# Two places instead of one between each sum of the RWKV-7 state chain and the product that reads it

## The chip, the cores and the metric

The kernel runs on one core of a Trainium2 chip. The metric is the device time of one launch in microseconds (us). Work is shared by TensorE (PE, matrix products), VectorE (DVE), ScalarE (ACT), GpSimd (POOL) and SyncE (SP, which issues most of the transfers).

## The reference

One layer of a hybrid decoder on 256 prompt tokens and 8 decode tokens, T = 264 columns, in 32-bit floats: a SwiGLU feed-forward block, a mixing layer in which attention heads and RWKV-7 heads stand side by side, a second SwiGLU block, and norms. The part that matters here is the RWKV-7 recurrence over the 256 prompt tokens, 16 heads of 64:

```python
def step(S, inp):
    r_t, lw_t, k_t, v_t, kk_t, a_t = inp
    sa = jnp.einsum('bhij,bhj->bhi', S, -kk_t)
    S = (S * jnp.exp(lw_t)[:, :, None, :] + sa[..., None] * (kk_t * a_t)[:, :, None, :]
         + v_t[..., None] * k_t[:, :, None, :])
    return S, jnp.einsum('bhij,bhj->bhi', S, r_t)
S, ys = lax.scan(step, S0.astype(jnp.float32), xs)
```

## The kernel before

All large products are weight products. `gemm` (its products have line 74 in the profile) goes through a weight tile in chunks of four 128 x 128 blocks: SP loads a chunk (`raw`), ScalarE rounds it to the fast product format (`hi`, line 127), VectorE or GpSimd forms the remainder (`lo`, line 58), and TensorE makes three products for each block, `hi` by `xh`, `hi` by `xl` and `lo` by `xh`, twelve for a chunk, each over 264 columns, into an `acc` bank of PSUM. There are 6 `raw`, 4 `hi` and 4 `lo` buffers, 3 `acc` banks and 5 banks with the tag `m` for all smaller products.

Between the two feed-forward blocks lies the mixing layer. Its projection `win` computes 38 tiles of 128 columns: tiles for the RWKV heads, then 4 tiles of keys and values, then 8 tiles of queries; after it the output projection (`in_wout`) adds in three passes. For the query tiles and the output projection the `lo` parts alternate between GpSimd and VectorE.

The smaller work of the mixing layer is written as Python generators in a list `tasks`. After each chunk, `gemm` calls `tick`, which lets every task in the list run on to its next `yield`. So a `yield` is a place in the program at which one chunk of products, and a step of every other task, stands between two parts of a task; `pause(n)` is n such places:

```python
def pause(n):
    for _ in range(n):
        yield
```

The tasks are: `prep`, one for each of 8 pairs of heads (decays, norms, the matrices within a block of 64 tokens); `chain`, one for each batch of two pairs, four in all; and `attend`, `dec_attend`, `dec_load` and `kvtask` for attention. The output projection waits (`drain`) for the tasks whose results a pass needs; `dec_load(1, ...)`, which starts the second decode attention, waits for the last chain.

`chain` first inverts triangular matrices (30 steps of two VectorE instructions, which write `st` and `Xt`), then forms, by products and copies, what the recurrence over four blocks of 64 tokens needs: `PT` (the map of a state over a block), `kr` (what reads the state), and, in the banks pN and pY, what each block adds to the state and the output by itself. Then comes the state chain, four sums with products between them: `N` scales pN; for c = 1, 2, 3 the products by `PT` and by `kr` read the state so far (`N` for c = 1, then `S`), and `S` is formed from it in two steps, `Z` (line 61) and `S` (line 61). Last, the outputs in pY are copied, the state is written (`out_wkvp`, line 697, issued by ScalarE's queue), `g2` is loaded and `gnorm` normalises the output.

The order in which each engine executes is not the program's: a planner assigns it, from a model of when operands are ready, and with the place in the program as priority. `tc.high_priority()` lifts the `hi` and `lo` steps of a chunk ahead of older work. Every engine then executes its own list in order, so an instruction that has to wait holds up what stands behind it.

Of the kernel before, what the change touches and what calls it, by code (L numbers as in the profile page):

```python
# [47 lines left out]
def body(tc, I, O):  # L48
# [11 lines left out]
    def stt(out, a, s, b, op0, op1):  # L60
        return V.scalar_tensor_tensor(out=out, in0=a, scalar=s, in1=b, op0=op0, op1=op1)  # L61
# [8 lines left out]
    def bc(ap, shape):  # L70
        return ap.broadcast_to(list(shape))

    def mm(out, lhsT, rhs, start=True, stop=True, **k):
        TE.matmul(out, lhsT, rhs, start=start, stop=stop, **k)  # L74
# [16 lines left out]
# [4 lines that stand above are left out]
    with ExitStack() as ctx:  # L95
# [17 lines left out]
        def mp():  # L113
            return pp.tile([P, 512], F32, tag="m", bufs=NM, name=uid("m"))
# [245 lines left out]
        def mixing_body(mx, n2, n3, XD):  # L360
# [3 lines left out]
            def ring(shape, tag, bufs):  # L364
                return mx.tile(list(shape), F32, tag=tag, bufs=bufs, name=uid(tag))
# [182 lines left out]
            def chain(bt):  # L548
# [114 lines left out]
                for k in range(n):  # L663
# [5 lines left out]
                               k + c == 0, c == 0, skip_group_check=True)  # L669
                tt(V, N, pN[:, :n * 256].rearrange("p (k c t) -> p k c t", k=n, c=4),  # L670
                   bc(wc[:, bt.p0:bt.p0 + n, :].unsqueeze(3), (P, n, 4, 64)), ALU.mult)
                yield
                S = N[:, :, 0, :]
                for c in range(1, 4):
                    ps = mp()
                    for k in reversed(range(n)):
                        for h in range(2):
                            r = HALF[h]
                            mm(ps[r, k * 64:k * 64 + 64], PT[r, k, c - 1, :], S[r, k])
                        for h in range(2):  # L680
                            r = HALF[h]
                            x = (k * 4 + c) * 64
                            mm(pY[HALF[1 - h], x:x + 64], S[r, k], bt.KR[k][r, 1, c, :], False, True,
                               skip_group_check=True)
                    Z, Sn = ring((P, n, 64), "Z", 2), ring((P, n, 64), "S", 3)
                    for k in range(n):
                        stt(Z[:, k], S[:, k], wc[:, bt.p0 + k, c:c + 1], N[:, k, c, :], ALU.mult, ALU.add)
                    for k in range(n):
                        stt(Sn[:, k], ps[:, k * 64:k * 64 + 64], wc[:, bt.p0 + k, c:c + 1], Z[:, k], ALU.mult, ALU.add)
                    S = Sn  # L690
                    yield
                for k in range(n):
                    for h in range(2):
                        A.copy(Ys[k][HALF[h], :NP], pY[HALF[1 - h], k * NP:(k + 1) * NP])
# [182 lines left out]
            for kind, i in SEQ:  # L877
                if kind == "b":
                    bt = newbatch(i)
                    for k in range(BATCH[i]):  # L880
                        p = bt.p0 + k
                        x = [shifted(2 + 3 * p + j, tmp()) for j in range(3)]
                        spawn(prep(p, bt, k, *x))
                    bat.append(spawn(chain(bt)))
                    bts.append(bt)
                    if len(bat) == len(BATCH):
# [206 lines left out]
```

## Time and profile before

| | |
|---|---|
| time, median of 3 runs | 1982.82 us (1982.39 to 1985.37) |
| the profiled execution | 1982.98 us, span 1981.2 us |
| busy: PE / DVE / ACT / POOL | 1960.8 / 1302.9 / 1064.1 / 347.8 us |
| the four state chains, first sum N at | 922.1, 993.5, 1047.8, 1117.8 us |
| projection and mixing layer, about | 700 to 1212 us of the span |

A time before an instruction is its start within the span. An entry of the list of waits gives who waited, for whom, microseconds in total, times, and the longest. In the order of time a bracket is the idle time of the engine just before the row, and the instruction that ended it by the profile; a product's end is modelled, so that products overlap in the rows.

### The profile page before, as it was taken

How to read it: one execution, taken by the hardware profiler on the slowest of the kernel's cores; microseconds unless marked ns; L12 is line 12 of the kernel's file. 1: busy time of each engine (PE TensorE's matmuls, PEld its weight loads, DVE VectorE, ACT ScalarE, POOL GpSimd, SP SyncE). 2: the span in 40 equal slices, each digit the busy share in tenths (PEclk: the TensorE clock that was granted, in tenths of full speed). 3: DMA queues.
4: the chain of work that ended last, by engine and by line, in shares of the span. 5: the costliest groups of instructions: out<-in, count | busy, mean ns of one | idle time of the engine just before them, and what ended most of it. 6: DMA issues, size and time to landing. Idle time of an engine off the chain costs nothing.

```text
span 1981.2 us, 45886 instructions
## 1 busy us (share of the span) xinstructions
PE 1960.8 (99%) x17212; PEld 1931.5 (97%) x17212; DVE 1302.9 (66%) x2542; ACT 1064.1 (54%) x2125; POOL 347.8 (18%) x453
## 2 busy tenths in 40 slices
PE   9999999999999999999999999999999999999997
PEld 9999999999999999999998899999999999999997
DVE  5865555655556567788877776866666666666655
ACT  5644444444444456777665755644444444444445
POOL 0401102010010112132133562210101001010112
PEclk9999999999999999999999999999999999999998
DMA  7666666665656667555656456565666666666664
GB/s 230 177 185 199 185 190 193 182 186 177 185 179 182 182 186 233 162 159 139 167 154 170 134 155 195 175 181 178 193 184 192 182 194 188 185 191 184 195 179 142
DMA packets 224880, 358.24 MB, mean 181 GB/s; under 512 B 38264, under 2 KB 79888, under 8 KB 224656
## 3 DMA queue, kind: packets, MB, share of 16 engines
q1 hardware_dynamic: 218768, 349.20, 59.7%
q10 hardware_dynamic: 5888, 6.11, 1.0%
q8 instruction: 135, 2.21, 0.4%
q14 instruction: 89, 0.73, 0.1%
HBM read 347.06 MB, written 10.22 MB: 180 GB/s over the span
## 4 chain that ended last, share of the span: by engine, by line
PE 96%; DVE 1%; DMA 1%; ACT 1%; issue 0%; SPq 0%; POOL 0%; DVEq 0%; ACTq 0%; POOLq 0%
PE acc L74 88%; PE m L74 7%; DMA raw<-in_gu 1%; DVE lo L58 0%; DVE Xt L58 0%; DVE st L58 0%; DMA TT<-sb 0%; DVE y L58 0%; DMA raw<-in_wout 0%; DMA raw<-in_win 0%; ACT t L68 0%; PE m L786 0%; PE m L522 0%; ACT L68 0%; ACT hi L127 0%
## 5 line engine op out<-in xcount | busy, mean ns | idle before, releaser
L127 ACT CAST hi<-raw 128x512 fp32r<-128x512 f32 (+2 forms) x1304 | 779.0, 602 | 809.5 <-PE acc L74 724.1
L58 DVE TENSOR_TENSOR lo<-raw,hi 128x512 fp32r<-128x512 f32 (+1 forms) x1248 | 854.6, 688 | 538.6 <-ACT hi L127 511.3
L74 PE MATMUL acc<-s,hi 128*128 128x264 f32 x5940 | 1109.1, 286 | 2.2 <-ACT hi L127 1.1
L74 PEld LDWEIGHTS acc<-s,hi 128*128 128x128 f32 x5940 | 923.1, 188 | 8.5 <-ACT hi L127 1.8
L74 PE MATMUL acc<-s,lo 128*128 128x264 f32 x2970 | 846.8, 286 | 0.3 <-DVE lo L58 0.2
L74 PEld LDWEIGHTS acc<-s,lo 128*128 128x128 f32 x2970 | 558.3, 188 | 3.6 <-issue 0.9
L74 PE MATMUL acc<-t,hi 128*128 128x264 f32 x2752 | 502.8, 284 | 0.0
L74 PEld LDWEIGHTS acc<-t,hi 128*128 128x128 f32 x2752 | 426.0, 188 | 0.0
L74 PE MATMUL acc<-t,lo 128*128 128x264 f32 x1376 | 388.7, 284 | 0.0
L58 POOL TENSOR_TENSOR t<-t,t 128x264 f32<-128x264 f32 (+1 forms) x148 | 151.1, 1021 | 1148.6 <-ACT hi L127 882.2
L74 PEld LDWEIGHTS acc<-t,lo 128*128 128x128 f32 x1376 | 258.1, 188 | 0.1
L74 PE MATMUL acc<-y,hi 128*128 128x264 f32 x648 | 123.9, 284 | 0.0
L74 PEld LDWEIGHTS acc<-y,hi 128*128 128x128 f32 x648 | 100.9, 188 | 0.2
L74 PE MATMUL acc<-y,lo 128*128 128x264 f32 x324 | 91.9, 284 | 0.0
L58 DVE TENSOR_TENSOR t<-acc,t 128x264 f32<-128x264 f32 x156 | 67.3, 432 | 36.2 <-PE acc L74 36.0
L58 POOL TENSOR_TENSOR lo<-raw,hi 128x512 fp32r<-128x512 f32 x56 | 73.6, 1316 | 57.4 <-ACT hi L127 36.0
L58 POOL TENSOR_TENSOR o<-o,o 128x264 f32<-128x264 f32 x43 | 36.1, 841 | 187.5 <-ACT o L68 183.5
L74 PE MATMUL acc<-o,hi 128*128 128x264 f32 x324 | 62.1, 281 | 0.0
L74 PEld LDWEIGHTS acc<-y,lo 128*128 128x128 f32 x324 | 60.9, 188 | 0.0
L61 DVE SCALAR_TENSOR_TENSOR s<-acc,s 128x264 f32<-128x264 f32 x96 | 40.5, 426 | 16.0 <-PE acc L74 15.5
L74 PEld LDWEIGHTS acc<-o,hi 128*128 128x128 f32 x324 | 49.9, 188 | 0.0
L74 PE MATMUL m<-s,hi 128*128 128x264 f32 x260 | 48.1, 285 | 0.0
(251 smaller groups left out, 1336.4 us busy)
## 6 DMA issues: line engine op xcount, KB each, us to landing
raw<-in_gu SPq DMA_DIRECT2D x688, 256.0 KB, 3.4
raw<-in_dn SPq DMA_DIRECT2D x224, 256.0 KB, 2.9
raw<-in_win SPq DMA_DIRECT2D x152, 256.0 KB, 3.5
raw<-in_dn SPq DMA_DIRECT2D x160, 192.0 KB, 2.7
raw<-in_wout SPq DMA_DIRECT2D x48, 256.0 KB, 3.3
raw<-in_wout SPq DMA_DIRECT2D x32, 128.0 KB, 3.0
s<-xsp SPq DMA_DIRECT2D x16, 132.0 KB, 3.8
ld<-in_sT SPq DMA_DIRECT2D x16, 128.0 KB, 3.7
```

Of the source, the lines that this page charges most:

```text
L58: return e.tensor_tensor(out=out, in0=a, in1=b, op=op)
L61: return V.scalar_tensor_tensor(out=out, in0=a, scalar=s, in1=b, op0=op0, op1=op1)
L74: TE.matmul(out, lhsT, rhs, start=start, stop=stop, **k)
L127: A.copy(hi[:, :w], raw[:, :w])
```

## The change

In `chain`, the `yield` after `N` and the `yield` at the end of each of the three rounds become `yield from pause(2)`. Nothing else changes: the instructions, their operands, the buffers and the loads stay as they are.

```diff
                 tt(V, N, pN[:, :n * 256].rearrange("p (k c t) -> p k c t", k=n, c=4),
                    bc(wc[:, bt.p0:bt.p0 + n, :].unsqueeze(3), (P, n, 4, 64)), ALU.mult)
-                yield
+                yield from pause(2)
                 S = N[:, :, 0, :]
                 for c in range(1, 4):
                     ps = mp()
...
                     for k in range(n):
                         stt(Sn[:, k], ps[:, k * 64:k * 64 + 64], wc[:, bt.p0 + k, c:c + 1], Z[:, k], ALU.mult, ALU.add)
                     S = Sn
-                    yield
+                    yield from pause(2)
```

## The prediction

> **What bounds the kernel now.** I read the page's busy line first, then the list of TensorE's waits, then the order of time around the sums of the state chain, then granted clock by short windows.
>
> ```profile
> PE 1960.8 (99%) x17212; PEld 1931.5 (97%) x17212; DVE 1302.9 (66%) x2542; ACT 1064.1 (54%) x2125; POOL 347.8 (18%) x453
> ...
> PE m L74 <- DVE st L58: 3.6, 1, 3.6
> PE m L74 <- DVE Xt L58: 2.2, 2, 1.2
> ```
>
> TensorE (PE) is busy 99% of the span, so a change that adds and removes no product can only give back time in which TensorE stands. The list of its waits (total us, times, longest) has about ten microseconds in the whole run; the two largest entries, 5.8 us, name VectorE (DVE). The next rows show where they lie: the sum N of each of the four chains, and the first products that read it. The bracket is TensorE's idle time before the row.
>
> ```profile
> 922.06 0.68 DVE L58 TENSOR_TENSOR N<-m,wc 128x512 f32<-128x512 f32 x1
> 922.89 0.27 PE L74 MATMUL m<-N,PT 64*64 64x64 f32 x2 [1.03 <-DVE Xt L58]
> ...
> 993.53 0.68 DVE L58 TENSOR_TENSOR N<-m,wc 128x512 f32<-128x512 f32 x1
> 994.36 0.27 PE L74 MATMUL m<-N,PT 64*64 64x64 f32 x2 [1.22 <-DVE Xt L58]
> ...
> 1047.81 0.68 DVE L58 TENSOR_TENSOR N<-m,wc 128x512 f32<-128x512 f32 x1
> 1048.64 0.27 PE L74 MATMUL m<-N,PT 64*64 64x64 f32 x2 [3.60 <-DVE st L58]
> ...
> 1117.76 0.69 DVE L58 TENSOR_TENSOR N<-m,wc 128x512 f32<-128x512 f32 x1 [0.41 <-PE m L74]
> 1119.91 0.27 PE L74 MATMUL m<-N,PT 64*64 64x64 f32 x2
> ```
>
> The releaser that is named (Xt, st: the doubling steps of the next batch's inverse) is only VectorE's instruction beside it; the product waits for N, which ends 0.15 us before it (1047.81 + 0.68 = 1048.49). Three chains pay 1.03, 1.22 and 3.60 us; the fourth pays nothing. The third pays twice, as the windows show (stretch, length, busy time of TensorE, weight load, DVE, ACT, POOL, then granted clock, DMA share, GB/s):
>
> ```profile
> 922.00:923.00 1.00, 0.11 (x5) 0.14 (x9) 1.00 (x5) 1.00 (x1) 0.00 (x0) 1.00 0.00 0
> 993.00:994.00 1.00, 0.14 (x2) 0.00 (x0) 0.91 (x4) 0.98 (x2) 0.21 (x2) 1.00 0.54 152
> 1049.00:1050.00 1.00, 1.00 (x14) 0.73 (x9) 0.90 (x6) 0.37 (x1) 0.00 (x0) 0.84 1.03 408
> 1050.00:1051.00 1.00, 1.00 (x9) 0.70 (x5) 1.00 (x5) 0.00 (x0) 0.70 (x1) 0.50 0.48 184
> 1051.00:1052.00 1.00, 1.00 (x6) 1.00 (x5) 1.00 (x8) 0.00 (x0) 0.20 (x1) 0.50 0.07 18
> 1052.00:1053.00 1.00, 1.00 (x6) 1.00 (x6) 1.00 (x8) 0.26 (x1) 0.00 (x0) 0.50 0.58 154
> 1053.00:1054.00 1.00, 1.00 (x22) 0.85 (x21) 0.93 (x5) 1.00 (x4) 0.51 (x1) 0.95 0.26 97
> ```
>
> In the first and second chain the granted clock stays at 1.00 across the wait. After the 3.60 us it falls to one half: the clock missing from 1.00 adds up to 0.16 + 3 x 0.50 + 0.05 = 1.71 us of work. So the three waits cost 1.03 + 1.22 + 3.60 + 1.71 = 7.56 us, and that is the ceiling of what later products can give back.
>
> **The change, part by part.** No instruction is added or removed. Of the four sums of each chain (N, then S for c = 1, 2, 3) each is now followed by two places where other work is put into the program, not one. A place is worth one chunk of the projection that is running: twelve products, three every 0.365 us by the next two rows, so 1.46 us, and whatever the other tasks emit there.
>
> ```profile
> 1043.78 0.28 PE L74 MATMUL acc<-s,lo 128*128 128x264 f32 x1
> ...
> 1044.14 0.28 PE L74 MATMUL acc<-s,lo 128*128 128x264 f32 x1
> ...
> 923.90 0.47 DVE L61 SCALAR_TENSOR_TENSOR S<-m,wc,Z 128x64 f32<-128x64 f32 x2
> ...
> 926.55 0.27 PE L74 MATMUL m<-S,PT 64*64 64x64 f32 x2
> ...
> 1125.13 0.47 DVE L61 SCALAR_TENSOR_TENSOR S<-m,wc,Z 128x64 f32<-128x64 f32 x2
> ...
> 1126.76 0.27 PE L74 MATMUL m<-S,PT 64*64 64x64 f32 x2
> ```
>
> *After S, c = 1 and 2.* The first S shown ends at 924.37, 2.18 us ahead of its product; the last, the nearest of all, 1.16 us ahead. None of these products has idle time in front. I take 0 here, from both sides: nothing stands that could be won, and the second chunk is work that is due anyway.
>
> *After N, third chain.* TensorE stops at 1048.64 - 3.60 = 1045.04 and N is ready 3.45 us later. What would now come in between is what stands behind the products today, if its operands are there:
>
> ```profile
> 1039.79 1.14 ACT L127 CAST hi<-raw 128x512 fp32r<-128x512 f32 x2
> 1041.00 1.27 POOL L58 TENSOR_TENSOR lo<-raw,hi 128x512 fp32r<-128x512 f32 x1 [1.29 <-ACT hi L127]
> 1044.35 0.68 DVE L58 TENSOR_TENSOR lo<-raw,hi 128x512 fp32r<-128x512 f32 x1
> ...
> 1050.22 0.68 DVE L58 TENSOR_TENSOR lo<-raw,hi 128x512 fp32r<-128x512 f32 x1
> ...
> 1049.03 0.33 PE L786 MATMUL m<-C,t 128*128 128x128 f32 x1
> ...
> 1049.51 1.53 PE L74 MATMUL m<-s,o 64*128 64x256 f32 x8
> ...
> 1132.05 0.92 PE L74 MATMUL m<-s,o 64*128 64x256 f32 x8
> ```
>
> Chunk operands alternate between VectorE and GpSimd here, so of the two hi casts at 1039.79 the first gets the lo that ends at 1045.03, the second the one of 1041.00: two chunks lie ready when TensorE stops. The transposes of attention (1049.03 to 1049.51, 0.48 us) and eight score products (0.85 us at full clock, from 0.92 less the overlap of the next row; 1.53 us above is the half clock) are also due. One chunk and both: 1.46 + 0.48 + 0.85 = 2.79 us, and 0.8 us of wait is left. If the chunk is planned behind the products after all, only 1.33 us is filled and 2.27 us stays. I take 2.79, since both operands are there by 1045.03.
>
> *The clock in the third chain.* A rest of 0.8 us is below 1.22 us, which left the clock at 1.00: 1.71 us comes back. A rest of 2.27 us lies between rows (1.22 no fall, 3.60 fall), so 0 or 1.71; it is nearer to 1.22, and I take 1.71.
>
> The Trainium skill, "TensorE: Matmul & The Clock Gate", Part 1 (the HAM clock gate), says that the array falls to half clock after a whole idle window of about 3.4 us, and that the windows run free of the kernel. By that, a rest of 2.27 us can never cost clock, and the 3.60 us can cover a whole window only when it lies well, so the 1.71 us could belong to the profiled execution alone. In the times, 1982.98 us for the profiled execution against a median of 1982.82 us speaks against this, as do half-clock stretches of 3.4 us that agree with the rule's length. By the rule's harsh reading the sum below would be 3.2 us, not 4.9.
>
> *After N, first and second chain.* Here the next chunk is not ready; what is late next is its lo.
>
> ```profile
> 923.18 0.68 DVE L58 TENSOR_TENSOR lo<-raw,hi 128x512 fp32r<-128x512 f32 x1
> 923.28 0.71 PE L74 MATMUL m<-ld,tw 65*128 65x128 f32 x4
> 924.31 0.60 PE L74 MATMUL acc<-s,hi 128*128 128x264 f32 x2
> ...
> 994.65 0.68 DVE L58 TENSOR_TENSOR lo<-raw,hi 128x512 fp32r<-128x512 f32 x1
> 994.75 0.71 PE L74 MATMUL m<-t,C 128*128 128x264 f32 x2
> 995.66 0.37 PE L74 MATMUL acc<-s,hi 128*128 128x264 f32 x1
> ```
>
> First chain: the prep products (923.28 to 924.31, 1.03 us) move into the gap, 921.86 to 922.89; the chunk's first lo product is due 0.24 us later, at 923.13, and its lo ends at 923.86, so 0.73 us of new wait stands against 1.03: a gain of 0.30, or 0.78 if the lo passes the two Z instructions (0.48) ahead of it. Second chain: prep products of 0.91 us from 993.14, lo product due at 994.29, lo ready at 995.33: 1.22 - 1.04 = 0.18, or 0.6. I take 0.5 and 0.4, between these ends because Z now comes later in the program.
>
> *What is moved later.* Each chain ends four places (5.8 us) later. With it go its copies on ScalarE, two state writes issued from ScalarE's queue (0.36 us each) and two loads of g2 on SP, which queue behind up to four more weight loads; the gate product that reads g2 moves as far. Who needs the chains: the projection's passes. The fourth is the tightest, because the second decode attention starts when it has ended:
>
> ```profile
> L870 POOL COPY o<-bk x8: 188/190/192, 1097.6 to 1162.8; 128x8 f32<-128x8 f32 x8
> ...
> 1176.51 0.43 DVE L58 TENSOR_TENSOR s<-acc,s 128x264 f32<-128x264 f32 x1 [0.36 <-PE acc L74]
> ```
>
> Its last copy ends near 1163; the last sum of the pass ahead of the one that needs it is at 1176.51. Cover of 13.5 us for 5.8 us, so 0; without the cover the drain would run with no chunk between its steps.
>
> *After that.* With chunks used earlier, the next lo casts of VectorE are due earlier while it is full (the windows above show it 0.90 to 1.00 busy). The third chunk's lo ends at 1050.90 and would be needed about 1050.7: 0.2 us. For later ones I have no row; between 0 and the whole 2.79 us won. I take 0.5 together, because a lo cast goes to the head of the queue once its hi exists.
>
> **Sum.** 0.5 + 0.4 + 2.8 + 1.7 - 0.5 = 4.9 us. The profiled execution took 1982.98 us (span 1981.2 and 1.8 around it): 1978.1; that execution lies 0.16 us over the median, so **1977.9 us**. What a measurement tells from no change here is about 0.2%, 4.0 us: the forecast is faster, by little more than that.
>
> **Rivals.** *The wait moves to the weights (same).* If VectorE really bounds 1040 to 1058, the 2.79 us comes back as waits for lo and one of them is long enough to halve the clock again: 4.9 + 0.5 - 2.8 - 1.7 = 0.9 us left, 1981.9; with the clock kept, 1980.2. For it: VectorE's full windows. Against: much of that work is doubling steps (Xt, st) that nobody waits for soon.
>
> *The change does not do what it says (same, 1982.8).* Each engine's order comes from a planner that goes by modelled readiness; between S products 20 or more chunk products stand already with one place. If it holds N ready early it can put the products where they are. Against: behind N just one chunk stood in three chains, which is what the program says.
>
> *Slower: PSUM banks.* pY holds one of five "m" banks for the whole chain, now four places longer. Prep takes two banks at a time, and one is emptied by this:
>
> ```profile
> 995.83 1.80 DVE L441 RECIPROCAL t<-m 128x264 f32<-128x264 f32 x1
> ```
>
> If TensorE stands for it, 1.8 us each: at two a chain 14.4 us, 1977.9 + 14.4 = 1992.3. It decides from five such waits on (4.9 + 4.0 = 8.9 us). Against: TensorE's waits show none today for a reader of a bank in these chains, with pY held just the same; for it: there are sixteen added places in which it could happen.
>
> **How the numbers follow.** Waits gone and clock kept: 0.53, with its own range from 1975.3 (7.56 us, all of it) to 1979.8 (only 1.33 us filled, 0.5 + 0.4 + 1.33 + 1.71 - 0.5 = 3.4 us, or the harsh clock rule). About a sixth of it, 0.09, falls short of 4.0 us. The wait moves: 0.24. Nothing happens: 0.10. Banks: 0.13. Faster 0.46 (0.44 of the first, 0.02 of the second by a re-planned order that wins elsewhere), same 0.41, slower 0.13. The range goes from 1975.3 to 1983.5: it takes in the first three and leaves out most of the bank case and little below.
>
> **What would show it.** Right: about 24 chunk products between the pY products and the first N products; brackets in front of them below 1 us; no window under 1.00 clock near the third chain; the two entries of the list of waits, 5.8 us, down to some 1 to 2 us. The S products as far behind their sums as now or farther. Wrong: new entries for TensorE on lo casts or on ScalarE and VectorE emptying banks; a half-clock stretch elsewhere; a drain at the pass near 1176.

## The result and the profile after

The changed kernel takes 1987.34 us (median of 21 runs, 1985.21 to 1989.67) against 1984.0 us for the kernel before in the same runs: a ratio of 1.0018, 95% interval 1.0012 to 1.0024. It is slower by 0.18%, where 0.25% faster was forecast, and lies above the forecast's range of 1975.3 to 1983.5 us. (The forecast started from the median of three runs, 1982.82 us; 21 runs put the kernel before at 1984.0.) Verdicts below are ratios to the kernel before on the same chip.

The page's busy line first, then the list of TensorE's waits between 850 and 1230 us, where the state chains lie, then TensorE's busy time in that stretch of both kernels, the kernel before first (length, busy time of TensorE, weight load, DVE, ACT, POOL, granted clock, DMA share, GB/s).

```profile
PE 1961.7 (99%) x17212; PEld 1931.1 (97%) x17212; DVE 1302.2 (66%) x2542; ACT 1065.9 (54%) x2125; POOL 348.9 (18%) x453
...
PE m L74 <- DVE st L58: 4.3, 2, 3.7
PE acc L74 <- DVE lo L58: 1.8, 2, 1.6
PE m L74 <- ACT TT L621: 1.4, 1, 1.4
PE acc L74 <- POOL s L58: 1.0, 1, 1.0
PE m L74 <- ACT PT L653: 0.7, 1, 0.7
PE m L74 <- DVE kr L58: 0.6, 1, 0.6
PE m L74 <- DVE S L61: 0.5, 1, 0.5
```

```profile
850.00:1230.00 380.00, 373.08 (x4118) 348.49 (x4117) 299.71 (x821) 251.83 (x635) 140.96 (x201) 1.00 0.56 158
```

```profile
850.00:1230.00 380.00, 369.13 (x4082) 343.69 (x4081) 295.15 (x815) 251.16 (x629) 143.00 (x201) 1.00 0.54 156
```

TensorE's busy time over the span is the same within 0.9 us (1960.8 and 1961.7). What grew is its idle time in the mixing layer: 380 - 373.08 = 6.92 us before, 380 - 369.13 = 10.87 us after, 3.95 us more. The span grew by 3.8 us (1981.2 to 1985.0). So the idle time of the mixing layer is as large as the whole loss; elsewhere 0.8 us less idle time before 700 us and the 0.9 us of busy time nearly cancel.

The waits one by one, in TensorE's order of time after the change (the bracket is its idle time before the row):

```profile
921.63 0.68 PE L74 MATMUL m<-la,ld 128*128 128x264 f32 x2 [0.54 <-DVE st L58]
...
922.86 0.27 PE L74 MATMUL m<-N,PT 64*64 64x64 f32 x2 [0.18 <-DVE Xt L58]
...
968.13 0.39 PE L74 MATMUL acc<-s,lo 128*128 128x264 f32 x1 [1.61 <-DVE lo L58]
...
1003.04 1.68 PE L74 MATMUL m<-kr,bk 64*128 64x128 f32 x16 [0.47 <-DVE S L61]
...
1032.17 1.52 PE L74 MATMUL m<-kr,TT 64*64 64x64 f32 x56 [1.39 <-ACT TT L621]
...
1043.64 0.94 PE L74 MATMUL m<-s,o 64*128 64x256 f32 x8 [3.73 <-DVE st L58]
1044.72 0.37 PE L74 MATMUL m<-N,PT 64*64 64x64 f32 x2
...
1109.28 0.70 PE L74 MATMUL m<-s,o 64*128 64x256 f32 x2 [0.74 <-ACT PT L653]
1110.57 0.89 PE L74 MATMUL m<-s,o 64*128 64x256 f32 x6 [0.60 <-DVE kr L58]
```

Around N the change won a little: first chain 0.54 + 0.18 instead of 1.03, second nothing instead of 1.22, third 3.73 and 0.14 instead of 3.60, so 4.59 instead of 5.85 us, 1.26 us less. Elsewhere it made new waits: lo casts 1.61 and 0.18, prep 0.27 and 0.47, the copies of TT 1.39, the fourth chain's score products 0.74 and 0.60, together 5.26 us. The waits at the first pass of the output projection are 0.97 instead of 1.03 us. The balance is +3.94 us.

The third chain's wait halves the clock as before, only some 5 us earlier (the seventh column, behind the length and the five engines, is the granted clock):

```profile
1044.00:1045.00 1.00, 0.86 (x17) 0.65 (x17) 1.00 (x5) 0.00 (x0) 0.00 (x0) 0.71 0.79 215
1045.00:1046.00 1.00, 1.00 (x19) 0.88 (x15) 0.90 (x6) 0.00 (x0) 0.00 (x0) 0.50 0.96 391
```

The clock falls to 0.50 within 1 us of the wait's end, and the stretch at half clock costs 1.71 us of work, as it did before; so the clock adds nothing to the loss.

### The profile page after: what moved, and what is told of

Read it like the earlier page. It is cut to its first block, busy times and chain, and to the rows that moved or that the text cites. A ratio compares the mean times of both kernels' runs of the same rounds, so it can differ in the third digit from the quotient of the medians.

```text
span 1985.0 us, 45888 instructions
## 1 busy us (share of the span) xinstructions
PE 1961.7 (99%) x17212; PEld 1931.1 (97%) x17212; DVE 1302.2 (66%) x2542; ACT 1065.9 (54%) x2125; POOL 348.9 (18%) x453
## 4 chain that ended last, share of the span: by engine, by line
PE 93%; DVE 3%; DMA 2%; ACT 1%; issue 1%; SPq 0%; POOL 0%; DVEq 0%; ACTq 0%; POOLq 0%
PE acc L74 86%; PE m L74 6%; DVE lo L58 1%; DMA raw<-in_gu 1%; DVE st L58 1%; DVE Xt L58 1%; DMA X<-sa 0%; DMA raw<-in_wout 0%; ACT hi L127 0%; DMA TT<-sb 0%; DVE y L58 0%; DVE kr L58 0%; DMA raw<-in_win 0%; DMA bk<-vnd 0%; ACT L68 0%
```

## The experiments

### One part of the change at a time

`n_only` doubles the place after N alone, `s_only` the three places after S alone, `n_first2` the place after N in the first two chains alone:

```diff
# n_only                        # s_only                       # n_first2
-                yield           -                    yield     -                yield
+  yield from pause(2)           +  yield from pause(2)         +  yield from pause(2 if bt.i < 2 else 1)
   S = N[:, :, 0, :]
```

> Only the place after N is doubled; the three after S stay single. Theory A (the planner fills the gap before N's products by modelled readiness, so a second place only swaps what stands in the gap): the waits at N change as in the changed kernel, about 0.7 + 0 + 3.7 us instead of 1.0 + 1.2 + 3.6, and without the later tail there are no new ones: 1 to 2 us faster than before. Theory B (the place after N itself is what costs, because attention's score products come ahead of N's products while the banks are held): new waits of 1 to 2 us appear in the last two chains and it is as slow as the changed kernel, +3 to +4 us. Theory C (every re-plan costs or wins by chance): anything from -4 to +4 us, with waits in places that have nothing to do with N.

> Only the three places after S are doubled; N keeps one. Theory A: all of the new waits of the changed kernel (lo casts 1.8, TT 1.4, others 0.7 us) come from the tail that is three places later, and nothing is won at N: slower than the changed kernel, +4 to +5 us. Theory B: N's place alone costs, so this is as before, within 1 us, with the waits 1.0, 1.2 and 3.6 us at N. Theory C: -4 to +4 us.

> The place after N doubled in the first two chains alone. In the kernel with N's place doubled in all four, the waits are 0.7 + 0.2 (first chain), 0.8 (second), 3.6 (third) and 1.6 us (a later wait for W in the fourth). If the loss of that kernel comes from the last two chains, where attention's score products move ahead of N's: the wait of 1.6 us goes and this is 0.5 to 1.5 us faster than before. If it comes from re-planning by chance: 1 to 4 us slower, with new waits outside of N.

Measured: `n_only` 1.0011 (1.0002 to 1.0020), `s_only` 1.0001 (0.9992 to 1.0010), `n_first2` 1.0016 (1.0007 to 1.0025). So the later tail costs nothing by itself, against theory A's expectation of +4 us, and N's place loses even where attention has no part in it. Theory B has `s_only` right, but by it `n_only` was to lose 3 to 4 us, and it loses 1.4. The two halves give 0.0012 together, the whole 0.0018: within the intervals they add up, but few of the waits do. `s_only` keeps N's waits (1.05, 1.55, 2.72 us) and has none of the lo or TT waits of the changed kernel; `n_only` has those of the first and the third chain again, a TT wait of 0.43 instead of 1.39 us, and others of its own:

```profile
922.56 0.68 PE L74 MATMUL m<-la,ld 128*128 128x264 f32 x2 [0.73 <-DVE st L58]
...
993.53 0.68 PE L74 MATMUL m<-C,t 128*128 128x128 f32 x4 [0.84 <-DVE st L58]
...
1052.29 0.94 PE L74 MATMUL m<-s,o 64*128 64x256 f32 x6 [3.60 <-DVE st L58]
...
1115.12 0.27 PE L74 MATMUL m<-BT,W 64*64 64x64 f32 x2 [1.55 <-ACT W L639]
```

In `n_first2` the third chain, with a single place, waits 4.37 us in front of N's products, and passes that the edit does not touch have new waits near 1091 (0.77, 0.58) and 1156 us (1.49); the half clock behind the 4.37 us lasts 6.8 us, not 3.4. That is theory C's mark, though C allowed anything from -4 to +4 us and so risked little.

### What a place elsewhere does

```diff
# place_kv: in kvtask, behind the store of each key and value tile
-                yield
+                yield from pause(2)
# place_end: in chain, behind everything else
                     mixed[p] = o
-                yield
+                yield from pause(2)
```

> A doubled place that has nothing to do with the state chain: after the store of each key and value tile. It shows what a re-plan alone does. If re-plans win or cost 2 to 4 us by chance, this is off by as much in either direction; if the loss of the changed kernel is of the chain's own making, this is within 1 us of before, with the same three waits at N.

> A doubled place at the very end of each chain, behind all of its work, so that only the second decode attention starts a place later. Same question as the doubled place at the key and value tiles: off by 2 to 4 us if re-plans alone do it, within 1 us of before if not.

`place_kv` 1.0016 (1.0007 to 1.0025), `place_end` 1.0002 (0.9993 to 1.0011). A place that has nothing to do with the state chain can cost as much as the change; the other one costs nothing that can be told. In `place_kv` the waits at N are close to those of before (1.00, 1.24, 3.82 us). Of 2.82 us more idle time in the mixing layer, 2.08 us are one new wait, for a softmax step of ScalarE:

```profile
1075.36 0.33 PE L786 MATMUL m<-C,t 128*128 128x128 f32 x1 [2.08 <-ACT t L68]
```

`place_end` has new waits too (1.16 and 1.38 us near 1143 and 1150) and a half clock of 6.8 us, but its time over all runs is that of the kernel before.

### The backlog of VectorE, and the banks

`pin_before`, `pin_after`, `pin_n` and `pin_s` queue the steps of the inverse (`st`) behind the newest N on VectorE, so that steps of later places can't stand ahead of N; places are single, all doubled, doubled after N, doubled after S. `bank_after` and `bank_before` put the two score tiles of prompt attention into `acc` banks; `pin_bank` is the changed kernel with both, `pin_bank1` both with single places.

```diff
# pin_*
-                tt(V, N, ...)
+                gate[:] = [tt(V, N, ...).ins]
...
-                    with tc.issue_after(cuts[0]):
+                    with tc.issue_after(cuts[0]), tc.issue_after(gate[0]) if gate else nullcontext():
                         tt(V, t, bc(X[:, s:s + 1, s + 1:], shp), bc(Y[:, :m, s:s + 1], shp), ALU.mult)
# bank_*
-                spp = [mp(), mp()]
+                spp = [acc(), acc()]
```

> The kernel before, with the steps of the next batch's inverse queued on VectorE behind the newest N instead of ahead of it; places stay single. If the waits at N are VectorE's backlog of these steps: N starts 1 to 3 us earlier against its pN products, the three waits shrink from 5.9 us to below 1.5 us in total, the half clock after the third (1.7 us) goes, 4 to 6 us faster than before. If N is late for another reason (its products, the kr sums, lo casts): the waits stay above 4 us and the time is within 2 us of before.

> The changed kernel with the same queueing of the inverse's steps behind N. If its third-chain wait of 3.7 us before the score products is a bank that the kr sums free late because of the same backlog: that wait falls below 1.5 us and the clock stays at 1.00 there; 4 to 5 us faster than the changed kernel, the new waits on lo and TT stay. If the score products wait for something else, the wait stays above 3 us and the time within 1.5 us of the changed kernel.

> Only N's place doubled, with the inverse's steps queued behind N. If the doubled place after N is worth having once the backlog is gone: waits in the chains below 4 us in total, 1 to 3 us faster than before. If what makes the queued version of the changed kernel quick is the later tail (the S places), this is like the single-place version with the same queueing, 2 to 4 us slower than before.

> Only the S places doubled, with the inverse's steps queued behind N. If the later tail is what helps the queued version: 1 to 3 us faster than before. If the place after N is what helps: 2 to 4 us slower than before, with the waits of the single-place version with the same queueing (lo 1.4, norm 1.9, pass start 2.4 us) still there.

> The changed kernel with the two score tiles of prompt attention in acc banks instead of m banks. If the 3.7 us in front of the third chain's score products are a wait for an m bank (four are held by the chain until its kr sums and N): the score products no longer wait; the same backlog of VectorE then shows in front of N's own products, 2.5 to 3.6 us, and the clock still halves there; the time stays within 2 us of the changed kernel. If the score products wait for data, their wait of 3 us or more stays where it is.

> The changed kernel with both remedies: the inverse's steps queued behind N, and the score tiles in acc banks. If both waits (VectorE's backlog and the held banks) are what the doubled places cost: waits in the mixing layer below 3.5 us, 2 to 4 us faster than before, the fastest version. If re-plans by chance decide: as the version with the queueing alone or slower, with waits elsewhere.

> Both remedies (steps queued behind N, score tiles in acc banks) with single places. If the doubled places are themselves worth something once their two hindrances are gone: this is 1 to 4 us slower than the version with both remedies and doubled places. If the remedies alone made that version quick: the same or faster, waits in the mixing layer below 5 us, 3 us or more faster than before.

> The kernel before with the score tiles in acc banks, nothing else. If banks matter only where the score products stand ahead of N's (doubled places): within 1 us of before, waits of 1.0, 1.2 and 3.6 us still in front of N's products. If the banks are a cost of their own: 1 us or more faster.

| places | as they are | steps behind N | score tiles in acc | both |
|---|---|---|---|---|
| single | 1 (before) | 1.0017 (1.0009 to 1.0026) | 1.0061 (1.0047 to 1.0075) | 1.0085 (1.0071 to 1.0099) |
| N doubled | 1.0011 (1.0002 to 1.0020) | 1.0043 (1.0030 to 1.0055) | | |
| S doubled | 1.0001 (0.9992 to 1.0010) | 1.0000 (0.9991 to 1.0008) | | |
| all doubled | 1.0018 (1.0012 to 1.0024) | 0.9992 (0.9983 to 1.0001) | 1.0001 (0.9992 to 1.0010) | **0.9980** (0.9971 to 0.9989) |

With the steps behind N the waits in front of N's first products go in `pin_after` (none over 0.12 us, against 5.85 us before) and shrink to one of 0.77 us in `pin_before`. In the third chain N started 5.23 us behind the end of the last product it reads in the kernel before, 5.49 us in the changed kernel, and 0.05 us in `pin_after`, where VectorE now waits for TensorE:

```profile
1041.09 0.69 DVE L58 TENSOR_TENSOR N<-m,wc 128x512 f32<-128x512 f32 x1 [0.41 <-PE m L74]
```

So N was late through VectorE's queue, not through its own products: this is shown. It made `pin_after` 0.26% quicker than the changed kernel, as expected. It did not make `pin_before` quick, which was to gain 4 to 6 us, because the time came back elsewhere, with the clock halved twice:

```profile
970.94 0.39 PE L74 MATMUL acc<-s,lo 128*128 128x264 f32 x1 [1.43 <-DVE lo L58]
...
1019.65 0.71 PE L74 MATMUL m<-sgl,ld 128*128 128x264 f32 x2 [1.93 <-DVE y L58]
...
1092.21 0.87 PE L74 MATMUL acc<-s,hi 128*128 128x264 f32 x3 [2.39 <-ACT s L917]
```

`pin_n` and `pin_s` missed both of their cases: one is 8.3 us slower than the kernel before, the other the same. So neither half of the places makes `pin_after` quick by itself.

The held banks show in the changed kernel's own trace: the score products start 0.05 to 0.15 us after the instruction that empties a bank of the chain. VectorE's and ScalarE's rows for that:

```profile
1042.88 0.61 DVE L58 TENSOR_TENSOR kr<-m,kr 128x192 f32<-128x192 f32 x2
...
1108.27 0.96 ACT L653 COPY PT<-m 64x384 f32<-64x384 f32 x2
...
1109.82 0.61 DVE L58 TENSOR_TENSOR kr<-m,kr 128x192 f32<-128x192 f32 x2
```

The kr sums end at 1043.49 and 1110.43, the score products start at 1043.64 and 1110.57; PT ends at 1109.23, and the first of them start at 1109.28. Those in front of the third chain's N products read, by their order, the second query tile, which had been written at 1031.60 (first row below, the changed kernel). With the tiles in `acc` banks (`bank_after`, the other rows) the same products run at 1031.02 and 1032.79, some 10 us ahead of N's, and VectorE's backlog shows in front of N's products, as expected:

```profile
1031.19 0.41 DVE L61 SCALAR_TENSOR_TENSOR o<-acc,rs 128x264 f32<-128x264 f32 x1
...
1031.02 0.70 PE L74 MATMUL acc<-s,o 64*128 64x256 f32 x4
...
1032.79 0.49 PE L74 MATMUL acc<-s,o 64*128 64x128 f32 x4
...
1042.72 0.27 PE L74 MATMUL m<-N,PT 64*64 64x64 f32 x2 [2.96 <-DVE N L58]
```

So it was the banks that held the score products. The kernel gained 0.17% on the changed one, 3.4 us where at most 2 were expected, of which the trace explains the smaller part: idle time in the mixing layer fell from 10.87 to 9.69 us, and the clock was still halved once.

`pin_bank` is the fastest of all, 1979.79 us against 1983.99 us for the kernel before, a little more than the 2 to 4 us that were expected. Its list of waits has no entry for N in the chains and its clock stays at 1.00 (windows of the mixing layer, and of the stretch of the third chain):

```profile
850.00:1230.00 380.00, 375.13 (x4129) 348.92 (x4128) 293.39 (x822) 255.11 (x635) 144.52 (x201) 1.00 0.56 159
1040.00:1060.00 20.00, 19.62 (x184) 16.68 (x183) 18.63 (x86) 14.28 (x47) 9.31 (x13) 1.00 0.47 135
```

4.87 us idle (expected below 3.5) and no half clock, against 6.92 us idle and 1.7 us of clock before. That is not the whole account, though: by the times of its hi casts this kernel is 1.5 us ahead of the kernel before near 1225 us and 3.4 us near 1946 us, so over half of the lead came in the second feed-forward block, where nothing was edited.

The same two remedies with single places cost 0.85%, and the banks alone 0.61%; both were expected within a few us of the kernels beside them, and all cases written down for them missed. Idle time in the mixing layer and clock give 3.9 and 3.4 us of the 11.8 us by which the profiled span of `bank_before` grew, and 5.0 and 6.8 of 15.1 us for `pin_bank1`; the rest is not explained. That score tiles in `acc` banks hold up the projection, which has only three, is a rival that no run separates. Neither remedy, nor the doubled places, has a value of its own: each is worth what the plan around it makes of it, and with both remedies the doubled places are worth some 21 us ((1.0085 - 0.9980) x 1984).

### Where a chunk really stands in the gap

`n4_b0`: four places after N in the first chain; in the executed order 17 chunk products then stand between pY's products and N's.

```diff
-                yield
+                yield from pause(4 if bt.i == 0 else 1)
```

> Four places after N in the first chain alone, single places elsewhere; by the planned order 17 chunk products now really stand between the pN products and N's products there. The forecast's own step: the 1.03 us in front of the first chain's products go, and the chunk's lo cast is late by 0.2 to 0.7 us in its place; the second and third chain keep 1.2 and 3.6 us; time within 2 us of before. If the step itself was wrong, the wait at N stays near 1 us although the chunk stands there.

One run, 1985.21 us, against a median of 1983.7 us before. In front of N's products of the first chain there is no wait, 0.55 us is left ahead of the prep products that moved into the gap; the second waits 0.60 and the third 3.52 us. So the step as such works where the chunk is there. New waits of 1.69 us (pass start, 1088) and 1.50 us (1152) stand against it, and the clock was halved for 6.8 and 3.4 us, where the kernel before has 3.4.

## Why the prediction was wrong

Term by term, in us: forecast 0.5 + 0.4 + 2.8 + 1.7 - 0.5 = 4.9 won; measured 0.31 + 1.22 - 0.27 + 0 - 5.26 (and 0.06 at the output projection) = -3.94. Two steps failed: what a place is worth, which cost the third and fourth term, and the price of moving everything behind it, the fifth, which is the largest. With the first step right and the second as measured, the change would have won next to nothing.

**The first step that failed: "A place is worth one chunk of the projection that is running".** The executed order has 11, 12, 11 and 0 chunk products between the pY products and N's first products before the change, and 3, 5, 0 and 0 after it, not 24. In the rows of the third chain above, the score products stand there and no chunk. The work that TensorE does in this gap was 1.52, 1.66 and 1.53 us in the three chains that waited, and is 1.82, 1.63 and 1.42 us now: the gap does not grow, so it does not reach to where VectorE really ends N. A likely reason, which no run tests: weight products are ready earlier than the chain's, so the plan has mostly used the chunks of both places by the time N's products come up, and it issues these when its model has N ready; one more place then only lets other tasks' products into the modelled gap. The rival "the change does not do what it says" had named this; it got 0.10, on the ground that one chunk stood there in three chains, "which is what the program says". That agreement did not outlast the edit, so it was no rule.

**First chain: right. Second chain: luck.** The prep products moved into the gap as said. First chain: 0.31 us won, forecast 0.30 to 0.78. Second: 1.22 us won, forecast 0.18 to 0.6, but not by more work in the gap (1.63 us, before 1.66): N started 1.00 us behind its last product instead of 2.98, because VectorE had fewer steps of the inverse left in front of it. The forecast took N's time as fixed.

**Third chain: wrong.** 0.8 us was to be left; 3.73 us is. The score products were counted as ready, by their operands; their output was not looked at. Each needs two of five `m` banks while the chain holds four (pP, pG, pN, pY). They waited for the bank that the kr sums empty, and these sums stand in the same backlog of VectorE as N. The bank rival had the resource right but looked at pY and prep; the place was N and attention, and the price 3.73 us, not 1.8.

**The clock: its price was right in this kernel, its threshold was not.** The clock still halved once, 1.71 us. For the case of a rest of 2.27 us the forecast took the wait as harmless, being nearer to 1.22 than to 3.60. `s_only` halved it after 2.72 us, `pin_before` after 1.93 us (rows below); but `place_kv` kept 1.00 across 2.08 us and `pin_n` across 2.01 and 2.14 us, so no length of a single wait divides the cases.

```profile
1020.00:1021.00 1.00, 1.00 (x7) 0.89 (x6) 1.00 (x2) 0.00 (x0) 0.88 (x1) 0.87 0.51 119
1021.00:1022.00 1.00, 1.00 (x6) 1.00 (x6) 1.00 (x3) 0.62 (x1) 0.00 (x0) 0.50 0.72 228
```

The Trainium skill's whole idle window of about 3.4 us ("TensorE: Matmul & The Clock Gate", Part 1) does not hold here, where 1.93 us of idle time were enough; the length does, since every stretch at half clock ahead of the kernels' last microseconds lasts 3.4 us or a multiple of it.

**The second step that failed, "What is moved later" and "After that": 0.5 us forecast, 5.26 us measured.** No cover ran out: the second decode attention was done in time. What was missed is that a place moved re-plans everything behind it, and that after a re-plan other instructions end just when, or just after, TensorE needs them; that the planner's model has VectorE and ScalarE quicker than they are would explain it, but is not shown. The fourth chain's 0.74 and 0.60 us are the banks again. `place_kv` puts a size on re-planning alone: 0.16% from a place that touches none of the steps argued about. The rivals held no losing case for that (0.02 was kept for an order that wins elsewhere), and the forecast of 0.25% was of its size.

What stays open: why just these waits (lo at 968, TT at 1032) came up. It was seen that the lo stood behind a 1.80 us reciprocal and prep sums of VectorE, and TT's copies behind softmax steps of ScalarE; which modelled time set them there wasn't tried. The mixing layer's idle time and the clock account for the changed kernel, `n_only` and `pin_before` within 0.3 us of span, though not for all the others. In most of them a slow drift through the second feed-forward block adds to it, from 1.9 us won in `pin_bank` to 2.6 us lost in `n4_b0` by the times of the hi casts, and its cause is open too.

## What to carry to other kernels

Where a planner orders the engines, a `yield` more is a change of priority, not of distance: look at the executed order between producer and consumer before pricing what will stand there, and count output banks with the operands. A wait of an in-order engine goes when the backlog ahead of its producer goes, but the time is only kept if no other instruction, planned to end just in time, is exposed instead: here the same edit was worth +0.18%, -0.25%, -0.60% and -1.04% of time, depending on other lines (the four pairs of the table's first and last row). Before believing a gain of 0.3%, move a place that should not matter and see what it does: here 0.16% at one place and nothing at another.

## What the runs showed of the hardware

The clock halved after a TensorE wait of 1.29 us (`bank_before`, the first two rows) and stayed at 1.00 across one of 2.14 us (`pin_n`, the last two):

```profile
1066.00:1068.00 2.00, 0.71 (x3) 0.30 (x2) 0.71 (x2) 1.99 (x4) 0.00 (x0) 0.97 0.90 199
1068.00:1070.00 2.00, 2.00 (x8) 1.06 (x8) 2.00 (x4) 0.56 (x2) 0.59 (x1) 0.50 0.55 189
...
1078.00:1080.00 2.00, 0.00 (x0) 0.00 (x0) 1.45 (x4) 1.97 (x5) 0.00 (x0) 1.00 0.55 102
1080.00:1082.00 2.00, 1.90 (x17) 1.59 (x18) 1.93 (x3) 1.07 (x4) 1.28 (x1) 1.00 0.90 255
```

In `pin_after` it halved after waits of 0.54 and 0.68 us within 2.7 us, among transposes and products of 32 x 32:

```profile
1022.55 0.27 PE L734 MATMUL m<-C,s 128*8 128x128 f32 x1 [0.54 <-DVE s L58]
1024.73 0.95 PE L74 MATMUL m<-s,o 64*128 64x256 f32 x6 [0.68 <-DVE y L61]
```

```profile
1025.00:1026.00 1.00, 1.00 (x8) 0.80 (x7) 1.00 (x1) 0.63 (x3) 1.00 (x2) 0.74 0.64 212
1026.00:1027.00 1.00, 1.00 (x6) 1.00 (x6) 1.00 (x3) 0.14 (x1) 1.00 (x1) 0.50 0.11 41
```

Where a wait lies decides part of it. In all sixteen traces the changes of the granted clock, up to the last fall near the end, are whole multiples of 3.41 us apart (in the kernel before, half from 1049.68 to 1053.09 us). Cut the mixing layer into stretches of that length from such a change: each of the eleven at full clock in which TensorE stood for 1.93 us or more was followed by half clock; the waits of 2.08 and 2.14 us were each split over two stretches; and with 1.16 to 1.89 us in one stretch both happened. What decides there is open; that products of small size count as idle in `pin_after` is a guess.

The half clock lasted 3.41 us and cost 1.71 us of work in most runs, but a single one lasted twice as long in `n_first2`, `place_end`, `n4_b0` and `bank_before`, and three times in `pin_bank1`.
